# A mixture of softmaxes: 64-row units with two heads per partition, all heads weighed on TensorE, half rows stored

## The chip, the cores and the metric

The kernel runs on one core of one Trainium2 chip. The metric is the device time of one execution in microseconds (us), the median of several runs. The kernel before took 806.44 us, the median of 3 runs from 806.37 to 809.75.

## The reference

For each of 32*128 = 4096 rows there are four heads of 4096 logits and four prior values. The result is the mean of the four softmaxes, weighed with the softmax of the prior:

```python
prior_probs = softmax(prior)                    # (32, 128, 4)
sm = exp(logits - logits.max(axis=-1, keepdims=True))
sm = sm / sm.sum(axis=-1, keepdims=True)        # (32, 128, 4, 4096)
out = np.sum(prior_probs[..., None] * sm, axis=2)   # (32, 128, 4096) float32
```

The logits are 268.4 MB, the result is 67.1 MB, all in float32.

## The kernel before

**Tiling.** A unit `u` is 128 rows, one row on each partition with all four heads, 8 MB; there are 32 units. Rows are taken in groups of 256 (`g`), and partition `p` has the rows 2p and 2p+1 of a group, one in each of two units (`j`). A unit comes in two loads of 4 MB (heads 0 and 1, heads 2 and 3), each into one of four slots of [128, 2, 4096]; a load has one packet of 32 KB per partition. The loads are issued from ScalarE's queue (`load`, L63 to L68).

**Per head** (`top`, L76): VectorE finds the negated maximum of 4096 values (L77), ScalarE replaces the values by their exponentials and sums them up (L80), VectorE takes the reciprocal of the sum (L86). For heads 0 to 2, GpSimd makes a diagonal matrix of reciprocal times prior (L89), and TensorE multiplies it with the exponentials in eight pieces of 512 columns, summed up over the heads in PSUM (L95). A float32 matmul is two instructions in the profile. [...]

**The fourth head** isn't on TensorE. For columns 0 to 3071, VectorE multiplies the head by its weight and adds the accumulator, in three pieces (`merge`, L107). For the last 1024 columns ScalarE copies the accumulator (L152), GpSimd weighs the head (L146) and adds the two (L160).

**Order.** Everything is issued in an order written out by hand (`tc.manual_schedule()`); each engine works through its own instructions in order, and waits are semaphores that follow from the buffers. In the loop over `u` (L141) the finishing of unit `w = u - 1` is put between the four heads of unit `u`. The load of the second half of unit u+1 is issued after the fourth head of w is used up (L164), that of the first half of unit u+2 at the end of the round (L177).

**Stores.** Two units share one output buffer [128, 2, 4096] of two; as the two rows of a partition lie next to each other in memory, a store of 4 MB has one contiguous run of 32 KB per partition (L167), and it covers all 128 partitions. It is issued on SP's queue. The last units are stored on their own (L169, L183).

**The prior** is loaded by SP (L114, 32 partitions of 2 KB), made into a softmax by VectorE and ScalarE, and transposed in 32 x 32 blocks into `pp`, so that each partition has the prior of its row as a scalar (L125 to L139).

Of the kernel before, what the change touches and what calls it, by code (L numbers as in the profile page):

```python
# [7 lines left out]
FP32 = mybir.dt.float32  # L8
AF = mybir.ActivationFunctionType
ALU = mybir.AluOpType  # L10
AX = mybir.AxisListType

P = 128
J = 2
BANK = 512


@with_exitstack
def kernel(
    ctx: ExitStack,  # L20
    tc: tile.TileContext,
    logits: bass.AP,
    prior: bass.AP,
    out: bass.AP,
):
    nc = tc.nc
    B, S, H, V = logits.shape
    R = P * J
    G = B * S // R
    U = G * J  # L30
    assert G * R == B * S and 2 * G == 32 and H == 4 and V == 8 * BANK


    lg = logits.rearrange("b s h v -> (b s) h v").rearrange("(g p j) h v -> g j p h v", p=P, j=J)
    ov = out.rearrange("b s v -> (b s) v").rearrange("(g p j) v -> g p j v", p=P, j=J)
    pv = prior.rearrange("b s h -> (b s) h").rearrange("(k r) h -> k r h", r=P)

    cpool = ctx.enter_context(tc.tile_pool(name="cpool", bufs=1))
    psum = ctx.enter_context(tc.tile_pool(name="psum", bufs=1, space=bass.MemoryType.PSUM))


    slots = [cpool.tile([P, 2, V], FP32, name=f"slot{i}") for i in range(4)]

    obufs = [cpool.tile([P, J, V], FP32, name=f"obuf{i}") for i in range(2)]
    acc = psum.tile([P, V], FP32, name="acc")

    ident = cpool.tile([P, P], FP32, name="ident")
    diag = [cpool.tile([P, P], FP32, name=f"diag{h}") for h in range(3)]
    pr = cpool.tile([2 * G, P, H], FP32, name="pr")
    pn = cpool.tile([2 * G, H, P], FP32, name="pn")  # L50
    pmax = cpool.tile([2 * G, P], FP32, name="pmax")
    pp = cpool.tile([P, J, H, 2 * G + 1], FP32, name="pp")
    nmax = [cpool.tile([P, U], FP32, name=f"nmax{h}") for h in range(H)]
    dsum = [cpool.tile([P, U], FP32, name=f"dsum{h}") for h in range(H)]
    rden = [cpool.tile([P, U], FP32, name=f"rden{h}") for h in range(H)]
    last = cpool.tile([P, U], FP32, name="last")

    DVE_COLS = 6 * BANK

    def slot(u, h):  # L60
        return slots[(2 * u + h // 2) % 4][:, h % 2]

    def load(u, half, cuts=(0, 2)):  # L63
        for a, b in zip(cuts, cuts[1:]):
            nc.scalar.dma_start(
                out=slots[(2 * u + half) % 4][:, a:b],
                in_=lg[u // J, u % J, :, 2 * half + a : 2 * half + b, :],
            )  # L68

    def obuf(u):  # L70
        return obufs[(u // J) % 2][:, u % J]

    def prob(u, h):
        return pp[:, u % J, h, 2 * (u // J) + 1 : 2 * (u // J) + 2]

    def top(u, h):  # L76
        nc.vector.tensor_reduce(  # L77
            out=nmax[h][:, u : u + 1], in_=slot(u, h), axis=AX.X, op=ALU.max, negate=True
        )
        nc.scalar.activation(  # L80
            slot(u, h), slot(u, h), AF.Exp, bias=nmax[h][:, u : u + 1],
            accum_out=dsum[h][:, u : u + 1],
        )

    def recip(u, h):
        nc.vector.reciprocal(rden[h][:, u : u + 1], dsum[h][:, u : u + 1])  # L86

    def matmuls(u, h):
        nc.gpsimd.tensor_scalar(  # L89
            out=diag[h], in0=ident, scalar1=rden[h][:, u : u + 1], scalar2=prob(u, h),  # L90
            op0=ALU.mult, op1=ALU.mult,
        )
        for b in range(V // BANK):
            cols = slice(b * BANK, (b + 1) * BANK)
            nc.tensor.matmul(  # L95
                acc[:, cols], lhsT=diag[h], rhs=slot(u, h)[:, cols],
                start=h == 0, stop=h == H - 2,
            )

    def weight(u):  # L100
        recip(u, H - 1)
        nc.gpsimd.tensor_mul(  # L102
            last[:, u : u + 1], rden[H - 1][:, u : u + 1], prob(u, H - 1)
        )

    def merge(u, lo, hi):
        nc.vector.scalar_tensor_tensor(  # L107
            out=obuf(u)[:, lo:hi], in0=slot(u, H - 1)[:, lo:hi], scalar=last[:, u : u + 1],
            in1=acc[:, lo:hi], op0=ALU.mult, op1=ALU.add,
        )  # L110

    with tc.manual_schedule():
        load(0, 0)
        nc.sync.dma_start(out=pr, in_=pv)  # L114
        load(0, 1)
        load(1, 0)
        load(1, 1)

        nc.gpsimd.memset(ident, 1.0)  # L119
        nc.gpsimd.affine_select(  # L120
            out=ident, in_=ident, compare_op=ALU.is_equal, fill=0.0, base=0,
            pattern=[[-1, P]], channel_multiplier=1,
        )

        nc.vector.reduce_max(pmax, pr, axis=AX.X)  # L125
        nc.vector.tensor_sub(pr, pr, pmax.unsqueeze(2).to_broadcast([2 * G, P, H]))  # L126
        nc.scalar.activation(pr, pr, AF.Exp)  # L127
        nc.vector.reduce_sum(pmax, pr, axis=AX.X)  # L128
        nc.vector.reciprocal(pmax, pmax)  # L129
        nc.vector.tensor_mul(  # L130
            pn.rearrange("k h r -> k r h"), pr, pmax.unsqueeze(2).to_broadcast([2 * G, P, H])
        )
        pq = pn.rearrange("k h (p j) -> k j h p", j=J)
        for t in range(P // 32):
            c = 1 - t // 2
            nc.vector.transpose(  # L136
                pp[32 * t : 32 * (t + 1), :, :, c : c + 2 * G],
                pq[:, :, :, 32 * (t % 2) : 32 * (t % 2 + 1)],
            )  # L139

        for u in range(U):  # L141
            w = u - 1
            top(u, 0)
            if w >= 0:
                weight(w)
                nc.gpsimd.tensor_scalar(  # L146
                    out=slot(w, 3)[:, DVE_COLS:], in0=slot(w, 3)[:, DVE_COLS:],
                    scalar1=rden[3][:, w : w + 1], scalar2=prob(w, 3),
                    op0=ALU.mult, op1=ALU.mult,
                )  # L150
                merge(w, 0, 2 * BANK)
                nc.scalar.copy(obuf(w)[:, DVE_COLS:], acc[:, DVE_COLS:])  # L152
            top(u, 1)
            recip(u, 0)
            if w >= 0:
                merge(w, 2 * BANK, 4 * BANK)
                merge(w, 4 * BANK, 6 * BANK)
            matmuls(u, 0)
            if w >= 0:
                nc.gpsimd.tensor_add(  # L160
                    obuf(w)[:, DVE_COLS:], obuf(w)[:, DVE_COLS:], slot(w, 3)[:, DVE_COLS:]
                )
                if u + 1 < U:
                    load(u + 1, 1, (0, 2) if u + 1 < U - 1 else (0, 1, 2))  # L164
                if w % J == J - 1:
                    eng = nc.sync if w < U - J - 1 else nc.scalar
                    eng.dma_start(out=ov[w // J], in_=obufs[(w // J) % 2])  # L167
                elif w == U - 2:
                    nc.sync.dma_start(out=ov[w // J, :, w % J], in_=obuf(w))  # L169
            top(u, 2)  # L170
            recip(u, 1)
            matmuls(u, 1)
            top(u, 3)
            recip(u, 2)
            matmuls(u, 2)
            if u + 2 < U:
                load(u + 2, 0)  # L177

        u = U - 1
        weight(u)  # L180
        for lo in (0, V // 2):
            merge(u, lo, lo + V // 2)
            nc.sync.dma_start(  # L183
                out=ov[u // J, :, u % J, lo : lo + V // 2], in_=obuf(u)[:, lo : lo + V // 2]
            )


# [28 lines left out]
```

## Time and profile before

| | |
|---|---|
| median of 3 runs | 806.44 us |
| the profiled execution | 805.12 us |
| its span, first to last instruction | 803.4 us |
| TensorE clock granted, mean | 0.973 |
| HBM read, written | 268.5 MB, 67.1 MB |
| loads of 4 MB: issue to landing, median | 21.9 us |
| stores of 4 MB | 23.7 us |
| stores of 1 MB, at the end | 3.9 us |

The page shows busy time by engine and by group of instructions. PE is TensorE, PEld its weight loads, DVE is VectorE, ACT ScalarE, POOL GpSimd, SP SyncE, which issues transfers. In the rows of 40 slices each digit is a busy share in tenths, and GB/s is what the 16 DMA engines moved. q10 is the queue of the transfers issued from ScalarE, q1 that of those issued from SP. Beside the page, the trace has a record for each packet (one contiguous run of a transfer on one DMA engine) with its start, duration, size and queue.

### The profile page before, as it was taken

The numbers are of one execution on the slowest core, as the hardware profiler recorded it, in microseconds if no ns is written. First come the engines' busy times: TensorE is split into PE (matmuls) and PEld (weight loads), VectorE is DVE, ScalarE is ACT, GpSimd is POOL, SyncE is SP. The second block draws the span as 40 slices with busy tenths as digits, with TensorE's granted clock in tenths as the row PEclk, the third lists the DMA queues.
The fourth block names the chain that finished last, engine by engine and source line by source line (L and its number), as shares of the span: only waits on it lengthen the run. The fifth ranks groups of instructions, "written<-read, shape, count | busy, mean of one in ns | idle before, by whom it ended". The sixth has DMA issues, their size and how long they took to land.

```text
span 803.4 us, 4541 instructions
## 1 busy us (share of the span) xinstructions
PE 691.1 (86%) x1536; PEld 295.3 (37%) x1536; DVE 689.6 (86%) x360; ACT 517.0 (64%) x289; POOL 158.6 (20%) x196
## 2 busy tenths in 40 slices
PE   0899898897998979979798998979989898897996
PEld 0344343333343434334343343333434333343442
DVE  6799898798889979799798898978889897898993
ACT  2776677575675756676666766656757666575672
POOL 0112222121221212211122211212212122121220
PEclk9999999998999999999999999989999999899999
DMA  9999999999999999999999999999999999999992
GB/s 395 427 432 389 420 443 414 438 426 438 416 424 428 427 426 437 423 440 437 425 434 427 432 427 438 427 436 421 423 432 432 433 426 434 430 404 439 425 392 106
DMA packets 12023, 335.90 MB, mean 418 GB/s; under 512 B 1344, under 2 KB 1344, under 8 KB 1376
## 3 DMA queue, kind: packets, MB, share of 16 engines
q10 hardware_dynamic: 9504, 272.63, 79.4%
q1 hardware_dynamic: 2496, 62.98, 18.4%
q8 instruction: 12, 0.20, 0.1%
q14 instruction: 11, 0.09, 0.0%
HBM read 268.50 MB, written 67.11 MB: 418 GB/s over the span
## 4 chain that ended last, share of the span: by engine, by line
DMA 45%; DVE 20%; PE 19%; issue 9%; POOL 6%; ACT 0%; POOLq 0%; DVEq 0%; ACTq 0%
DMA slot<-in_logits_dram 45%; PE acc L95 19%; DVE nmax L77 17%; POOL obuf L160 4%; DVE obuf L107 3%; POOL diag L89 1%; DVE rden L86 1%; POOL last L102 0%; POOL slot L146 0%; ACT obuf L152 0%; POOLq L89 0%; ACT slot L80 0%; DVEq L107 0%; POOLq L146 0%; POOLq L160 0%
## 5 line engine op out<-in xcount | busy, mean ns | idle before, releaser
L95 PE MATMUL acc<-slot,diag 128*128 128x512 f32 x1536 | 691.1, 609 | 104.9 <-POOL diag L89 104.9
L77 DVE TENSOR_REDUCE nmax<-slot 128x1 f32<-128x4096 f32 x128 | 563.9, 4411 | 61.7 <-DMA slot<-in_logits_dram 61.7
L80 ACT ACTIVATE slot<-slot,nmax 128x4096 f32<-128x4096 f32 x128 | 474.9, 3710 | 203.7 <-DVE nmax L77 182.5
L95 PEld LDWEIGHTS acc<-slot,diag 128*128 128x128 f32 x1536 | 295.3, 195 | 499.8 <-issue 349.0
L107 DVE SCALAR_TENSOR_TENSOR obuf<-slot,last,acc 128x1024 f32<-128x1024 f32 (+1 forms) x95 | 120.5, 1295 | 37.8 <-PE acc L95 23.8
L89 POOL TENSOR_SCALAR diag<-ident,rden,pp 128x128 f32<-128x128 f32 x96 | 42.9, 447 | 490.9 <-DVE rden L86 476.6
L160 POOL TENSOR_TENSOR obuf<-obuf,slot 128x1024 f32<-128x1024 f32 x31 | 73.7, 2376 | 0.0
L152 ACT COPY obuf<-acc 128x1024 f32<-128x1024 f32 x31 | 31.4, 1012 | 63.9 <-PE acc L95 63.9
L146 POOL TENSOR_SCALAR slot<-slot,rden,pp 128x1024 f32<-128x1024 f32 x31 | 37.0, 1194 | 0.0
L102 POOL TENSOR_TENSOR last<-rden,pp 128x1 f32<-128x1 f32 x32 | 6.1, 189 | 139.7 <-DVE rden L86 139.7
L80 ACT ACTIVATION_READ_ACCUMULATOR slot<-slot,nmax 128x1 f32 x128 | 23.9, 187 | 0.0
L86 DVE RECIPROCAL rden<-dsum 128x1 f32<-128x1 f32 x128 | 19.6, 153 | 3.8 <-ACT slot L80 3.8
L125 DVE TENSOR_REDUCE pmax<-pr 32x128 f32<-32x512 f32 x1 | 0.7, 673 | 4.7 <-DMA pr<-in_prior_dram 4.7
L127 ACT ACT_TABLE_LOAD x1 | 1.3, 1283 | 3.2 <-issue 3.2
L136 DVE STREAM_TRANSPOSE pp<-pn 32x256 f32<-32x256 f32 x4 | 1.7, 434 | 0.1
L127 ACT ACTIVATE pr<-pr 32x512 f32<-32x512 f32 x1 | 0.6, 628 | 1.6 <-DVE pr L126 1.6
L128 DVE TENSOR_REDUCE pmax<-pr 32x128 f32<-32x512 f32 x1 | 0.7, 674 | 0.7 <-ACT pr L127 0.7
L130 DVE TENSOR_TENSOR pn<-pr,pmax 32x512 f32<-32x512 f32 x1 | 1.0, 1017 | 0.0
L129 DVE RECIPROCAL pmax<-pmax 32x128 f32<-32x128 f32 x1 | 0.9, 941 | 0.0
L126 DVE TENSOR_TENSOR pr<-pr,pmax 32x512 f32<-32x512 f32 x1 | 0.7, 679 | 0.0
L120 POOL TENSOR_SCALAR_AFFINE_SELECT ident<-ident 128x128 f32<-128x128 f32 x1 | 0.3, 292 | 0.1
L119 POOL MEMSET ident<- 128x128 f32 x1 | 0.2, 204 | 0.3 <-POOLq L200 0.3
(4 smaller groups left out, 0.4 us busy)
## 6 DMA issues: line engine op xcount, KB each, us to landing
slot<-in_logits_dram ACTq DMA_DIRECT2D x63, 4096.0 KB, 21.9
out_dram<-obuf SPq DMA_DIRECT2D x14, 4096.0 KB, 23.7
slot<-in_logits_dram ACTq DMA_DIRECT2D x2, 2048.0 KB, 13.4
out_dram<-obuf ACTq DMA_DIRECT2D x1, 4096.0 KB, 23.7
out_dram<-obuf SPq DMA_DIRECT2D x1, 2048.0 KB, 7.8
out_dram<-obuf SPq DMA_DIRECT2D x2, 1024.0 KB, 3.9
pr<-in_prior_dram SPq DMA_DIRECT2D x1, 64.0 KB, 3.8
```

The costliest lines, as they stand in the source:

```text
L77: nc.vector.tensor_reduce(out=nmax[h][:, u : u + 1], in_=slot(u, h), axis=AX.X, op=ALU.max, negate=True)
L80: nc.scalar.activation(slot(u, h), slot(u, h), AF.Exp, bias=nmax[h][:, u : u + 1], accum_out=dsum[h][:, u : u + 1],)
L86: nc.vector.reciprocal(rden[h][:, u : u + 1], dsum[h][:, u : u + 1])
L89: nc.gpsimd.tensor_scalar(out=diag[h], in0=ident, scalar1=rden[h][:, u : u + 1], scalar2=prob(u, h), op0=ALU.mult, op1=ALU.mult,)
L95: nc.tensor.matmul(acc[:, cols], lhsT=diag[h], rhs=slot(u, h)[:, cols], start=h == 0, stop=h == H - 2,)
L102: nc.gpsimd.tensor_mul(last[:, u : u + 1], rden[H - 1][:, u : u + 1], prob(u, H - 1))
L107: nc.vector.scalar_tensor_tensor(out=obuf(u)[:, lo:hi], in0=slot(u, H - 1)[:, lo:hi], scalar=last[:, u : u + 1], in1=acc[:, lo:hi], op0=AL ...
L127: nc.scalar.activation(pr, pr, AF.Exp)
L136: nc.vector.transpose(pp[32 * t : 32 * (t + 1), :, :, c : c + 2 * G], pq[:, :, :, 32 * (t % 2) : 32 * (t % 2 + 1)],)
L146: nc.gpsimd.tensor_scalar(out=slot(w, 3)[:, DVE_COLS:], in0=slot(w, 3)[:, DVE_COLS:], scalar1=rden[3][:, w : w + 1], scalar2=prob(w, 3), o ...
L152: nc.scalar.copy(obuf(w)[:, DVE_COLS:], acc[:, DVE_COLS:])
L160: nc.gpsimd.tensor_add(obuf(w)[:, DVE_COLS:], obuf(w)[:, DVE_COLS:], slot(w, 3)[:, DVE_COLS:])
```

## The change

A unit `n` is now 64 rows, 4 MB, one load: partition 2m + q has the heads 2q and 2q+1 of row m, 32 KB in one run. There are 64 units, five slots of 32 KB per partition, and all loads are on SP's queue. For `i` = 0 and 1 a unit has one maximum and one exponential over 128 partitions, which now cover two heads of 64 rows each.

TensorE weighs all four heads: the stationary operand `wt` is 128 x 64, with the weight of partition 2m + q in column m, so that the contraction adds the two heads of a row, and the two `i` are summed up in PSUM. The columns of the result are cut in two: the half `c` = 0 goes to PSUM partitions 0 to 63, the half `c` = 1 to partitions 64 to 127, each a matmul of its own on its own half of the array's columns. There are two accumulators of 128 x 2048. VectorE's merges and GpSimd's large instructions are gone; ScalarE copies the whole accumulator of a unit to SBUF in one instruction (`evict`).

The copy leaves half a row on a partition. So a group of two units is stored by two transfers of 1 MB (`store`), each from 64 partitions, with runs of 8 KB. They are issued from ScalarE's queue. The stores of the last four groups (`HOLD`) are issued on SP's queue behind the last load; the last two groups use a free slot as their buffer (`home`). The prior's load moves to ScalarE's queue.

```diff
-    lg = logits.rearrange("b s h v -> (b s) h v").rearrange("(g p j) h v -> g j p h v", p=P, j=J)
-    ov = out.rearrange("b s v -> (b s) v").rearrange("(g p j) v -> g p j v", p=P, j=J)
+    lg = logits.rearrange("b s h v -> (b s) h v").rearrange(
+        "(g m j) (q i) v -> g j m q (i v)", m=M, j=J, i=Q
+    )
+    ov = out.rearrange("b s v -> (b s) v").rearrange("(g m j) v -> g m j v", m=M, j=J)
...
-    slots = [cpool.tile([P, 2, V], FP32, name=f"slot{i}") for i in range(4)]
-    obufs = [cpool.tile([P, J, V], FP32, name=f"obuf{i}") for i in range(2)]
-    acc = psum.tile([P, V], FP32, name="acc")
+    slots = [cpool.tile([P, Q, V], FP32, name=f"slot{i}") for i in range(SLOTS)]
+    obuf = cpool.tile([P, 2, J, W], FP32, name="obuf")
+    accs = [psum.tile([P, W], FP32, name=f"acc{i}") for i in range(2)]
...
+    def load(n):
+        src = lg[n // J, n % J]
+        if n < N - 1:
+            nc.sync.dma_start(out=slots[n % SLOTS], in_=src)
+        else:
+            for i in range(Q):
+                nc.sync.dma_start(
+                    out=slots[n % SLOTS][:, i], in_=src[:, :, i * V : (i + 1) * V]
+                )
...
+    def weigh(n, i):
+        nc.vector.reciprocal(rden[i][:, n : n + 1], dsum[i][:, n : n + 1])
+        wt = wts[n % 2][i]
+        nc.gpsimd.tensor_scalar(
+            out=wt, in0=sel, scalar1=rden[i][:, n : n + 1],
+            scalar2=pp[:, n % J, i, n // J : n // J + 1], op0=ALU.mult, op1=ALU.mult,
+        )
+        for b in range(W // BANK):
+            for c in range(2):
+                nc.tensor.matmul(
+                    accs[n % 2][c * M : (c + 1) * M, b * BANK : (b + 1) * BANK],
+                    lhsT=wt,
+                    rhs=slots[n % SLOTS][:, i, c * W + b * BANK : c * W + (b + 1) * BANK],
+                    start=i == 0, stop=i == Q - 1,
+                )
+    HOLD = G - 4
+    def home(g):
+        if g < G - 2:
+            return obuf[:, g % 2]
+        return slots[(N - 5) % SLOTS][:, g % 2].rearrange("p (j w) -> p j w", j=J)
+    def evict(n):
+        nc.scalar.copy(home(n // J)[:, n % J], accs[n % 2])
+    def store(g, js=slice(0, J)):
+        eng = nc.scalar if g < HOLD else nc.sync
+        for c in range(2):
+            eng.dma_start(
+                out=ov[g, :, js, c * W : (c + 1) * W], in_=home(g)[c * M : (c + 1) * M, js]
+            )
...
+        for n in range(N):
+            w = n - 1
+            top(n, 0)
             if w >= 0:
+                weigh(w, 1)
+                if w + SLOTS < N:
+                    load(w + SLOTS)
+            top(n, 1)
+            weigh(n, 0)
             if w >= 0:
+                evict(w)
+                if w == N - SLOTS:
+                    for g in range(HOLD, w // J):
+                        store(g)
+                if w % J == J - 1 and (w // J < HOLD or w >= N - SLOTS):
+                    store(w // J)
+        n = N - 1
+        store(n // J, slice(0, 1))
+        weigh(n, 1)
+        evict(n)
+        store(n // J, slice(1, 2))
```

## The prediction

> **What bounds the kernel now.** I read the page's busy times and slices first, then the queues, then stretches of the span, then the groups for single durations. The page's rows of totals, slices and queues:
>
> ```profile
> PE 691.1 (86%) x1536; PEld 295.3 (37%) x1536; DVE 689.6 (86%) x360; ACT 517.0 (64%) x289; POOL 158.6 (20%) x196
> ...
> DMA  9999999999999999999999999999999999999992
> GB/s 395 427 432 389 420 443 414 438 426 438 416 424 428 427 426 437 423 440 437 425 434 427 432 427 438 427 436 421 423 432 432 433 426 434 430 404 439 425 392 106
> ...
> q10 hardware_dynamic: 9504, 272.63, 79.4%
> q1 hardware_dynamic: 2496, 62.98, 18.4%
> ```
>
> No compute engine is full, but the 16 DMA engines are in 39 of 40 slices: 79.4% and 18.4% of 803.4 us are 785.7 us of packets per engine. The stretches (columns: the stretch, its length, busy time and count of PE, PEld, DVE, ACT, POOL, then clock, DMA share, GB/s) show where the rest lies:
>
> ```profile
> 400.00:500.00 100.00, 90.43 (x204) 38.66 (x203) 88.01 (x47) 65.98 (x39) 20.88 (x26) 0.98 1.00 430
> ...
> 760.00:780.00 20.00, 18.68 (x45) 8.04 (x44) 19.03 (x10) 15.09 (x9) 4.59 (x5) 1.00 0.94 400
> 780.00:790.00 10.00, 10.00 (x25) 4.50 (x24) 5.75 (x5) 7.60 (x4) 1.08 (x3) 1.00 0.32 134
> 790.00:795.00 5.00, 5.00 (x13) 2.13 (x13) 2.33 (x1) 0.00 (x0) 0.00 (x0) 1.00 0.00 2
> 795.00:803.40 8.40, 0.99 (x3) 0.17 (x1) 2.36 (x2) 0.00 (x0) 0.00 (x0) 0.83 0.61 250
> ```
>
> The middle is transfer and nothing else (share 1.00). The idle DMA is in the end: 20*0.06 + 10*0.68 + 5 + 8.4*0.39 = 16.3 us, while the last unit is computed. So two things decide: what one packet costs, and what DMA does in the last 20 us. That the chain of waits names PE and DVE beside DMA says little here, as transfers are queued behind transfers throughout.
>
> The trace's packet records give the price of a packet on its engine: 32 KB takes 1213 ns (10th to 90th percentile, loads and stores alike), 16 KB 611, 8 KB 309 (median 314 in the last stores), so 9 ns per packet beside the bytes. In the records an engine that has both queues filled takes one load packet and one store packet in turn.
>
> **The compute, part by part.** The durations are these rows:
>
> ```profile
> L95 PE MATMUL acc<-slot,diag 128*128 128x512 f32 x1536 | 691.1, 609 | 104.9 <-POOL diag L89 104.9
> L77 DVE TENSOR_REDUCE nmax<-slot 128x1 f32<-128x4096 f32 x128 | 563.9, 4411 | 61.7 <-DMA slot<-in_logits_dram 61.7
> L80 ACT ACTIVATE slot<-slot,nmax 128x4096 f32<-128x4096 f32 x128 | 474.9, 3710 | 203.7 <-DVE nmax L77 182.5
> ...
> L152 ACT COPY obuf<-acc 128x1024 f32<-128x1024 f32 x31 | 31.4, 1012 | 63.9 <-PE acc L95 63.9
> ```
>
> A new unit moves one 4 MB load. At the DMA price it takes 803.4/64 = 12.5 us. DVE: 2*4.41 + 2*0.15 = 9.1 us (the 120.5 us of merges go). ACT: two exponentials with their read-outs, 2*(3.71 + 0.19), and a copy of 128x2048, estimated at twice 1.01 less a little, 1.9: 9.7 us, plus two 0.33 us store issues in every second unit. POOL: two small multiplies below 0.45 each; its 110.7 us of large ones go. All are below 12.5, so what they lose or gain lies beside the transfers and is worth nothing until the last load.
>
> PE: 16 matmuls of 64 columns, two instructions each; the row of back-to-back ones shows 20.87 us for 48, 0.435 each. If the two column tiles run beside each other a unit takes 16*0.435 = 7.0 us, if not 32*0.435 = 13.9, above 12.5. The trace has no column tile; both ends are kept, and I take the first, since the tiles have weights, outputs and columns of their own. [...]
>
> Waits: the last matmuls of a unit now stand behind the next unit's first reduction, so a slot comes free about 4.4 + 0.2 + 0.5 + 3.5 = 9 us (12 with serial tiles) after the next load has landed. Three loads, 37 us, are queued then; that covers it. On SP only loads wait, and stores have left that queue until the end. The PSUM copy waits for the store of two groups before, issued some 37 us earlier; with alternating packets it takes 16*(1.213 + 0.310) = 24.4 us. If that cover were gone, the exponentials behind the copy on ACT would wait, and loads two slots later. The preamble's weights move to ACT's queue and pass loads packet by packet; about 2 us late at most, covered by five loads.
>
> **The transfers.** Per engine: loads 512*1.213 = 621.1 us, as now; stores 512 packets of 8 KB at 0.310 = 158.7 instead of 128 at 1.213 = 155.3, so +3.5. The stalls of single packets (records above 1213 ns) were 8.0 us per engine, other gaps about 4, the first packet starts at 2.2.
>
> In the end the change wins: stores of the last four groups (64 packets an engine, 19.8 us) are held behind the last load. So the last load lands at T = 2.2 + 621.1 + 448*0.310 + 8 + 4 = 774.2. Then follow reduction (the first half's ends about T + 3.8), second reduction to 8.4, exponential to 12.8 (ACT also has a copy and one exponential ahead), reciprocal and weights 0.6, 8 matmuls 3.5, copy 1.9, store of 1 MB about 4 (3.9 for one of that size in the page): T + 23.5. The held stores would fit under it, if they run at 0.310 a packet.
>
> **What I don't believe is that price.** Every large transfer before covers 128 partitions; each new store covers 64. The only narrower transfer in the trace is the prior's: 32 partitions, 32 packets of 2 KB at the start. Alone such packets took 81 to 85 ns; with twelve to fifteen of them in flight, 98 to 146, median of all 89.5, and together they never moved more than about 240 GB/s, against 16*32768/1213 = 432 for the 128-partition loads. So engines that serve a narrow range of partitions seem to get in each other's way, by 1.0 to 146/82 = 1.78. A gain is excluded: no packet of 32 KB is faster than 1211 ns. For 8 KB that is 310 to 552 ns.
>
> - Between loads, where a store packet is a fifth of an engine's cycle (310 of 1523 ns) and engines are spread, I take the median, 89.5/84 = 1.07: 448*0.021 = 9.4 us; ends 0 and 448*0.242 = 108.
> - Behind the last load all engines do nothing but stores, all on the same half at a time; there I take the upper end: 64*0.552 = 35.3 us, with 2 us to land 37.3 instead of 23.5; the compute is then covered by the stores.
>
> Sum: 774.2 + 9.4 + 37.3 = 820.9 us of span. The profiled execution of before took 805.12 for a span of 803.4, 1.7 more, and stands 1.3 below the median of 806.44. **Forecast 822.6 us.**
>
> [...]
>
> **Rivals.**
> - **Narrow stores cost nothing** (other side). Prices stay at 0.310, the end is compute: 774.2 + 23.5 + 1.7 = 799.4 us, 0.7% below the profiled execution. For it: 17 of the 32 prior packets took 91 ns or less, and a load packet between two stores may give time to read ahead. It decides as long as the narrow packets lose under about 10 ns between loads and the held stores stay under 24 us.
> - **Engines in step.** If they do their store packets at the same moment, the 1.78 holds between loads too: 774.2 + 108 + 37.3 + 1.7 = 921; halfway 867. For it: at 100 us the records show 14 of 16 engines within 120 ns of each other. Against: at 700 us they are spread over the whole 1213.
> - **Column tiles run in turn.** PE then bounds: 2048*0.435 = 891 us, from 22.6 us (first matmul now) and 6 for the last copy and store: 920 + 1.7 = about 921.
>
> **How the numbers follow.** Narrow stores with a moderate price (812 to 870 us): 0.45. They cost nothing (797 to 806): 0.38. In step, beyond 870: 0.08. Tiles in turn: 0.09. The range 797 to 870 holds the first two, 0.83; the forecast's own is 812 to 870. About 0.5% is what a measurement of this kernel can tell from no change: under 802.4 I put 0.30 (most of the second case), within 802.4 to 810.5 0.08, above 0.62.
>
> **What would show it.** Packet records of 8 KB: near 310 ns throughout would refute the forecast; 330 between loads and 500 to 620 behind the last load bear it out. The GB/s of the last 40 us: about 420 or about 240. The chain that ended last: stores under the forecast, DVE, ACT and PE under the first rival. PE's back-to-back matmuls: 16 instructions in 3.5 us or in 7. DMA share below 0.95 in the middle would mean that a wait I called covered isn't, and the whole working would be wrong.

## The result, and the profile after

The changed kernel took 794.35 us (median of 4 runs, 793.69 to 795.03) beside 806.40 for the kernel before in the same job: a ratio of 0.9841, 95% interval 0.9814 to 0.9867. It is faster by 1.6%. The prediction had 822.6, a range of 797 to 870, and 0.62 for slower; the time lies below the range. Its profiled execution took 794.60 us for a span of 792.9.

The page of the changed kernel, its totals, slices, queues and chain:

```profile
PE 544.3 (69%) x2048; PEld 159.6 (20%) x2048; DVE 573.3 (72%) x268; ACT 600.1 (76%) x322; POOL 51.1 (6%) x135
...
DMA  9999999999999999999999999999999999999997
GB/s 375 441 414 431 430 426 429 433 431 428 433 436 433 434 434 431 429 427 437 429 431 429 431 434 431 433 436 430 433 432 432 427 432 427 432 431 438 432 386 234
...
q1 hardware_dynamic: 10544, 276.83, 81.9%
q10 hardware_dynamic: 8112, 58.79, 17.6%
...
DMA 76%; PE 10%; DVE 10%; issue 1%; POOL 1%; ACT 1%; SPq 0%; POOLq 0%
```

The chain of the kernel before:

```profile
DMA 45%; DVE 20%; PE 19%; issue 9%; POOL 6%; ACT 0%; POOLq 0%; DVEq 0%; ACTq 0%
```

Three things differ from before. The middle is smoother: from the fourth slice to the last but two the rate stands at 426 to 438 GB/s, where before it went down to 389, 414 and 404. The last slice moves 234 GB/s in place of 106. And the chain that ended last goes through the loads for 76% of the span, where it was 45%. No compute engine is over 76% busy; ACT has 600 us.

The groups behind the compute terms, and the transfers (last number: us from issue to landing):

```profile
L91 PE MATMUL acc<-slot,wt 128*64 128x512 f32 x2048 | 544.3, 689 | 236.6 <-POOL wt L84 236.5
...
L106 ACT COPY obuf<-acc 128x2048 f32<-128x2048 f32 x60 | 110.7, 1845 | 0.0
...
slot<-in_logits_dram SPq DMA_DIRECT2D x63, 4096.0 KB, 38.0
out_dram<-obuf ACTq DMA_DIRECT2D x56, 1024.0 KB, 25.5
```

A load lands 38.0 us after its issue, about the time of three loads, its own among them; that is the queue that the prediction counted on.

The stretches of the end (stretch, length, PE, PEld, DVE, ACT, POOL, then clock, DMA share, GB/s):

```profile
760.00:770.00 10.00, 8.54 (x40) 2.55 (x38) 10.00 (x5) 9.55 (x6) 0.79 (x2) 1.00 1.00 383
770.00:775.00 5.00, 3.62 (x19) 1.05 (x16) 2.33 (x2) 5.00 (x3) 0.39 (x1) 1.00 1.00 338
775.00:780.00 5.00, 4.96 (x26) 1.50 (x24) 0.17 (x1) 3.13 (x3) 0.39 (x1) 1.00 0.88 282
780.00:785.00 5.00, 0.87 (x6) 0.00 (x0) 0.00 (x0) 1.87 (x1) 0.00 (x0) 1.00 0.96 274
785.00:792.90 7.90, 0.00 (x0) 0.00 (x0) 0.00 (x0) 0.00 (x0) 0.00 (x0) 0.56 0.49 151
```

The last load lands at about 765. From there the DMA engines are busy (share 1.00, 0.88, 0.96), but move 270 to 340 GB/s: the share counts a packet that takes long as busy, and only GB/s tells that it does.

The packet records say the same by packet. "Long" is the sum of what packets of 8, 16 and 32 KB took above 309, 611 and 1213 ns, per DMA engine; "idle" is time with no packet from the first to the last, per engine. "Between loads" are the store packets ahead of the held ones:

```
kernel                        8 KB between loads       8 KB behind the last load   long, us   idle, us
before                        none                     median 314 (1 MB stores)    8.4        16.7
changed                       median 309, mean 309.9   mean 397, a tenth over 632  7.8        4.8
changed, wide held stores     mean 309.9               mean 311                    1.9        5.1
changed, two groups held      mean 309.9               median 627, mean 562        10.4       5.2
before, wide 8 KB stores      mean 309.8               -                           2.3        11.9
changed, three slots          mean 347                 mean 399                    77         30
```

So the narrow stores cost nothing between loads while the load queue is filled, and 28% more (397 ns against 309) behind the last load.

### The profile page after: what moved, and what is told of

It is laid out like the page before. It is cut to its first block, busy times and chain, and to the rows that moved or that the text cites. A ratio compares the mean times of both kernels' runs of the same rounds, so it can differ in the third digit from the quotient of the medians.

```text
span 792.9 us, 5418 instructions
## 1 busy us (share of the span) xinstructions
PE 544.3 (69%) x2048; PEld 159.6 (20%) x2048; DVE 573.3 (72%) x268; ACT 600.1 (76%) x322; POOL 51.1 (6%) x135
## 4 chain that ended last, share of the span: by engine, by line
DMA 76%; PE 10%; DVE 10%; issue 1%; POOL 1%; ACT 1%; SPq 0%; POOLq 0%
DMA slot<-in_logits_dram 76%; PE acc L91 10%; DVE nmax L74 9%; POOL wt L84 1%; ACT slot L77 0%; ACT slot L106 0%; SPq L65 0%; DVE rden L82 0%; POOLq L84 0%
## 5 line engine op out<-in xcount | busy, mean ns | idle before, releaser
L91 PE MATMUL acc<-slot,wt 128*64 128x512 f32 x2048 | 544.3, 689 | 236.6 <-POOL wt L84 236.5
L91 PEld LDWEIGHTS acc<-slot,wt 128*64 128x64 f32 x2048 | 159.6, 157 | 620.4 <-POOL wt L84 315.4
L106 ACT COPY obuf<-acc 128x2048 f32<-128x2048 f32 x60 | 110.7, 1845 | 0.0
L84 POOL TENSOR_SCALAR wt<-sel,rden,pp 128x64 f32<-128x64 f32 x128 | 50.3, 393 | 725.3 <-DVE rden L82 725.3
L106 ACT COPY slot<-acc 128x2048 f32<-128x2048 f32 x4 | 7.4, 1850 | 2.8 <-PE acc L91 2.8
## 6 DMA issues: line engine op xcount, KB each, us to landing
out_dram<-obuf ACTq DMA_DIRECT2D x56, 1024.0 KB, 25.5
```

The lines of the kernel that those rows point to most:

```text
L84: nc.gpsimd.tensor_scalar(out=wt, in0=sel, scalar1=rden[i][:, n : n + 1], scalar2=pp[:, n % J, i, n // J : n // J + 1], op0=ALU.mult, op1= ...
L91: nc.tensor.matmul(accs[n % 2][c * M : (c + 1) * M, b * BANK : (b + 1) * BANK], lhsT=wt, rhs=slots[n % SLOTS][:, i, c * W + b * BANK : c * ...
L106: nc.scalar.copy(home(n // J)[:, n % J], accs[n % 2])
```

## The experiments

The theory on record was that a store from 64 partitions makes its packets longer, a little between loads and by 1.78 behind them. The trace after had refuted the first half of it; the rivals that were left concern why, what the end costs, and where the 6 us of long packets in the middle went.

**How many slots.** In both, the two last groups use a buffer of their own:

```diff
-SLOTS = 5
+SLOTS = 4
```

> The changed kernel with four slots in place of five; the last two groups use a buffer of their own. Theory of depth: the 6 us of long packets that the change removed went because its load queue is never short; with four slots two loads (25 us) are still queued when a slot comes free about 10 us after the next landing, so long packets stay near 2 us per engine and the time at 794 to 796 us. Rival: it is the fifth slot that does it; then the stalls of 6 to 8 us of the kernel before come back, 799 to 802 us.

Measured: 794.46 us (794.26 to 794.99), ratio 0.9875 (0.9835 to 0.9915), as the theory of depth has it; a load lands 25.9 us after issue, and long packets in the middle are 1.9 us (2.2 with five). The fifth slot is worth nothing.

```diff
-SLOTS = 5
+SLOTS = 3
```

> The changed kernel with three slots. Theory of depth: one load (12.4 us with its share of stores) is queued when a slot comes free 9 to 10 us after a landing, and 1 to 2 us pass from issue to the first packet, so the queue runs short often: long packets or idle engines of 5 to 30 us, 800 to 825 us. Rival (depth is of no account, the stalls of before came from the size of its store packets): long packets stay near 2 us and the time below 797 us.

Measured: 887.38 us, ratio 1.1017 (1.0958 to 1.1077), far more than either forecast. Its page:

```profile
DMA  9999999999999999999999999999999999999798
GB/s 383 394 374 404 377 357 385 374 385 381 394 393 391 366 399 368 367 375 363 395 385 387 385 376 401 376 380 368 382 404 395 374 374 367 403 403 402 315 377 262
```

DMA is still at nine tenths up to the last slices, but at 360 to 400 GB/s. By the packet records engines were idle for 30 us, and load packets were long by 52 us per engine, store packets by 23. Four fifths of the long time in the middle lies in packets that began within 6 us of a moment at which at least two engines had no packet; 42% of all packets began there. The loads show it more sharply. The first five aside, 28 of 58 sent their first packet less than 1.5 us after they were issued, so that hardly anything was queued ahead of them. The first 16 packets of these 28 make 13.4 of the 16.3 us by which the first 16 of all 58 were long. An empty queue costs more than the gap: the packets after it are long too.

**Narrow stores of 32 KB in the kernel before.**

```diff
-                    eng.dma_start(out=ov[w // J], in_=obufs[(w // J) % 2])
+                    for c in range(2):
+                        rows = slice(c * 64, (c + 1) * 64)
+                        eng.dma_start(out=ov[w // J][rows], in_=obufs[(w // J) % 2][rows])
```

> The kernel before with each 4 MB store cut into two of 64 partitions, packets of 32 KB as before. [...] Rival, that a narrow store is free as long as load packets stand between (an engine reads ahead): packets stay at 1213 ns and the time within 806 +- 4 us.

Measured: 844.06 us, ratio 1.0482 (1.0435 to 1.0529): slower by 39 us, as a price on narrow packets would have it, but most of the loss isn't in them. Store packets are long by 9.8 us per engine, the wide load packets by 33.6, and idle time in the middle grows from 2.3 to 7.2 us. Where load and store packets alternated, nearly all of both kept 1213 ns (the records from 491 to 499 us, about 430 GB/s). A possible chain is that narrow stores that stand alone slow the engines unevenly, a load is complete with its slowest engine, the next is issued late, and the queue runs empty. It fits that 21 of 59 loads sent their first packet less than 2.5 us after their issue, where the kernel before has 12. The chain is argued, not shown.

**Wide stores of 8 KB in the kernel before.**

```diff
+                    for c in range(2):
+                        cols = slice(c * V // 2, (c + 1) * V // 2)
+                        eng.dma_start(
+                            out=ov[w // J][:, :, cols], in_=obufs[(w // J) % 2][:, :, cols]
+                        )
```

> The kernel before with each 4 MB store cut into two halves of the columns: packets of 8 KB, all 128 partitions. If the stalls of before came from 32 KB store packets that halve the loads' share, they shrink by 4 to 6 us and the time is 804 to 806 us with 3.5 us for 9 ns on each of 5376 more packets. If they came from a load queue that runs short, they stay and the time is 808 to 811 us.

Measured: 800.05 us (796.36 to 802.11), ratio 0.9923 (0.9893 to 0.9953). The kernel before went from 800.8 to 810.5 in that job. This is below both forecasts. In the profiled execution, the fastest (796.36), long packets fell from 8.4 to 2.3 us per engine; idle time fell too, from 16.7 to 11.9, most of it in the end, which neither theory had. Smaller store packets alone are worth about half of the whole change.

The record of issues ties the two theories together. In the kernel before, 12 of 59 loads sent their first packet less than 2.5 us after their issue, and the first packets of these 12 make 1.95 of the 2.1 us by which the first packets of all 59 were long. With stores of 8 KB it is 2 loads of 58, and most follow 4 to 9 us after their issue; in the changed kernel nearly all follow after 21 us or more. So with 32 KB store packets the load queue does run short, and part of the long time lies there.

**The same, narrow as well** (four stores, halves of rows and of columns):

> The kernel before with each 4 MB store cut in four: halves of the partitions and halves of the columns, so narrow and with packets of 8 KB. If narrow packets are free whenever load packets stand between, only those behind the last load of a burst lose: 800 to 806 us, at most 6 above the wide 8 KB version (800.05). If the loss of the narrow 32 KB version (844) came from being narrow alone, whatever the packet: 830 to 850 us.

Measured: 802.92 us, ratio 0.9967 (0.9940 to 0.9994), as the first forecast has it. Narrow and 8 KB costs 0.4% beside wide and 8 KB, by two ratios whose intervals just meet; narrow and 32 KB costs 5%. Size of packet and width of transfer have to be seen together.

**Fewer groups held.**

```diff
-    HOLD = G - 4
+    HOLD = G - 2
```

> The changed kernel with only the last two groups' stores held behind the last load. The last load lands 32 packets * 0.309 = 9.9 us later; the compute behind it, 17 us to the last copy and 4 for the last store, then covers the 32 held packets per engine even at 0.62 us each (19.8 us). Theory that the changed kernel's gain is its filled end: the time rises to 797 to 799 us. Rival, that holding is of no account because the narrow stores at the end lose what they fill: 793 to 795 us.

Measured: 797.45 us (797.22 to 797.71), ratio 0.9888 (0.9859 to 0.9917), as forecast: holding two more groups is worth 3.1 us. The records put these in long packets (10.4 us per engine for 7.8), not in idle time (5.2 and 4.8): the end is filled in both. The 32 held packets of each engine took 562 ns in the mean, yet most hid beside the compute: the last copy ends at 788.7 us, 7.3 before the end of the span.

**Held stores made wide.** Two transfers of 64 partitions become one of 128, packets of 8 KB, 32 KB apart in memory as before:

```diff
...
+        if g >= HOLD:
+            eng.dma_start(out=ow[g // 2, g % 2, :, js], in_=home(g)[:, js])
+            return
...
```

The values of these groups then stand in other places of the result. This version, the next one and the one with three slots and wide stores serve for the time alone.

> The changed kernel, but the last four groups' stores cover all 128 partitions in one transfer, with packets of 8 KB and the same pitch of 32 KB per partition in memory; for that the half rows of these groups go to other places of the result (permuted). [...] Rival, that stores without loads between run into a limit of the memory, narrow or not: packets stay long and the time at 793 to 795 us.

Measured: 789.06 us (788.77 to 789.10), ratio 0.9784 (0.9760 to 0.9808), within the 787 to 790 expected if it is the narrow range of partitions that makes the held packets long. Its end:

```profile
770.00:775.00 5.00, 3.63 (x18) 1.06 (x16) 1.81 (x2) 5.00 (x3) 0.39 (x1) 1.00 1.02 429
775.00:780.00 5.00, 4.96 (x24) 1.35 (x20) 0.16 (x1) 2.60 (x3) 0.39 (x1) 1.00 0.68 287
```

429 GB/s where the changed kernel has 338, then a share of 0.68, as engines have nothing left to store. Held packets took 311 ns in the mean. The last copy ends at 782.3 us and the span 4.8 us later; in the changed kernel it ends at 782.8, and stores go on for another 10.1. So the 23.0 us from the last load to the end are the compute's and the last store's.

**Held stores narrow, in one contiguous stretch of memory each.**

> The changed kernel, but each narrow store (64 partitions) of the last four groups goes to one contiguous stretch of the result, partition after partition at a pitch of 8 KB in place of 32 KB (permuted). [...] Rival, that the pitch in memory makes 16 engines meet in the same place: packets of 309 ns, 787 to 790 us.

Measured: 794.40 us, ratio 0.9850 (0.9826 to 0.9875); held packets 399 ns in the mean, as in the changed kernel (397). It is the range of partitions that counts, not the pitch in memory. Nor is it the size of a transfer: the 1 MB stores at the end of the kernel before, over 128 partitions, kept a median of 314 ns.

Narrow stores that have the engines to themselves run at about half the rate: with two groups held, three quarters of the 512 packets took 500 ns or more, the median 627, twice 309 and a little, and the stretch from 782 to 786 us moved 211 GB/s, where the wide held stores moved 429 (770 to 775 us). Why a narrow range does this, no run shows. Packets that stand between wide ones pay nothing of it: 309.9 ns in the mean of 7168.

**Column tiles one after the other.**

```diff
-        for b in range(W // BANK):
-            for c in range(2):
+        for c in range(2):
+            for b in range(W // BANK):
```

> The changed kernel with the loops over pieces and column tiles swapped: all matmuls of the first tile, then all of the second. If tiles run beside each other only when neighbours in the order are of different tiles, a burst of 16 instructions takes 16 * 0.435 = 7.0 us in place of 3.65, PE needs 13.9 us per unit against 12.4 for the transfers, and the time is 900 to 930 us. If TensorE looks far enough ahead to overlap them all the same, 793 to 795 us.

Measured: 793.93 us, ratio 0.9845 (0.9808 to 0.9883). The time is the rival's, but the burst is neither's: TensorE overlaps the tiles still, if less. The timelines of PE, first the changed kernel, then this one:

```profile
764.12 3.65 PE L91 MATMUL acc<-slot,wt 128*64 128x512 f32 x16 [0.73 <-POOL wt L84]
```

```profile
411.62 10.64 PE L91 MATMUL acc<-slot,wt 128*64 128x512 f32 x32 [2.34 <-POOL wt L84]
```

That is 0.228 us per instruction and 0.333, beside 0.435 in the kernel before. The second burst ran at a granted clock of 0.86 (410 to 422 us); another of this version, at 1.00 (423 to 435 us), took 9.81 us, 0.307 an instruction. At the full clock the gain is 1.9 and 1.4 times. That it is overlap, and not a cheaper instruction of 64 columns, the records of the changed kernel show: two instructions start 6 ns apart, and the next two 0.43 us later, the distance between single instructions of 128 columns before. At 10.6 us a unit PE still stays under the 12.3 of the transfers.

**Three slots, all stores wide.**

> The changed kernel with three slots and all stores over 128 partitions (half rows go to other places of the result, permuted). Theory that the loss of the three-slot version (887) is an empty load queue and the slow start after it, which has nothing to do with narrow stores: 865 to 890 us. Rival, that narrow stores running alone while no load is queued cause it: 800 to 830 us.

Measured: 848.10 us in the profiled execution, which is used here, and 872.04 in the only other. The 848.10 lie in neither forecast. The profiled execution has 27 us of idle and 38 us of long load packets per engine, and store packets of 309.4 ns. Of the 93 us that three slots lose, narrow stores then make about 40 (887.38 to 848.10), of which 5 are the end that wide stores fill (794.35 to 789.06); the greater part comes without them. Here too the first packets of loads that found the queue empty are the long ones: 23 loads of 58, sent within 1.5 us of their issue, make 12.0 of 12.9 us.

**Versions meant to be better.** With three groups held, the last three loads in halves, and the last copy split:

```diff
-    HOLD = G - 4
+    HOLD = G - 3
...
-        if n < N - 1:
+        if n < N - 3:
...
-        evict(n)
+        half = W // 2
+        nc.scalar.copy(home(n // J)[:, n % J, :half], accs[n % 2][:, :half])
+        nc.vector.tensor_copy(home(n // J)[:, n % J, half:], accs[n % 2][:, half:])
```

> A version meant to beat the changed kernel: three groups' stores held in place of four, the last three loads cut in halves so that VectorE starts on each half as it lands, and the last copy split between ScalarE and VectorE. VectorE's last reduction ends about 2 us earlier, the last copy 1 us shorter, 4.95 us of narrow stores go under the loads, so the last load lands 5 us later: 790 to 793 us. If the end is bound by the narrow stores alone and not by the compute: 792 to 795.

Measured: 793.26 us (792.95 to 793.31), ratio 0.9855 (0.9824 to 0.9885): about 1 us under the changed kernel, which the intervals of the two ratios don't tell apart. The forecast of 790 to 793 was missed by little; the time is that of an end bound by the narrow stores.

> The same with four groups held, as in the changed kernel. If the end of the changed kernel is bound by the held narrow stores, the earlier compute buys at most 1 us: 793 to 794.5 us. If it is bound by compute: 790.5 to 792.

Measured: 794.50 us, ratio 0.9874 (0.9843 to 0.9905), as the first forecast has it: an earlier compute buys nothing while the narrow stores end last.

## Why the prediction was wrong, point by point

- **The bound** was read rightly in the main: transfers before and after, and compute in their shadow, but for the 12 of 59 loads that came late in the kernel before. The copy took 1.85 us (1.9 estimated), PE's burst 3.65 (3.5), the wide end 23.0 (23.5, though the steps listed for it add up to 22.8). The rival of serial tiles did not come: 2048 instructions kept PE busy for 544 us.
- **The failed step: "the median, 89.5/84 = 1.07" between loads.** Worth 9.4 us in the sum; measured nothing (309.9 ns). The row it came from, the prior's load, was narrow packets with nothing between them, in the first us of the kernel. It could speak for the end at most, and not for a queue in which every second packet is a wide one. Nor do its records show a price of crowding: of the 18 packets that started with ten or more of them in flight, 13 took 81 to 91 ns, and of the seven that started with five or fewer, three took 98. The first rival named a reason, time to read ahead; whether that is the mechanism no run shows, only that 8 KB packets between loads are free.
- **"The stalls of single packets were 8.0 us per engine", carried over unchanged.** Worth 5.8 us: 2.2 were left in the middle. The prediction didn't ask when they came. In the trace before, about 6 of the 8 us lie in eleven clusters of six or more long packets within 3 us, mostly where transfers began or ended. The wide 8 KB version shows that the size of the store packets decides whether they come. The records fit a reason: an engine takes one packet of each queue in turn (a group's stores landed in 25.5 us, where 16 pairs of 1.52 us are 24.4), so a 32 KB store packet takes half of the engine from the loads while a store lasts, an 8 KB one a fifth, and with 32 KB the load queue ran short for 12 of 59 loads. Why a packet becomes long there is open.
- **"Other gaps about 4":** too much, worth 3.5. Packets of the two queues overlap a little, and nearly nothing was lost.
- **The end: "64*0.552 = 35.3 us".** That narrow packets get longer there was right (311 ns when wide), the size wrong: 64 held packets took 397 ns in the mean, 25.4 us, and the end 28.0 in place of 37.3. Only a quarter of them took 500 ns or more; that engines come out of the loads at different times may be why, and no run tests it. With the stores wide the end is 23.0.

These four are 9.4 + 5.8 + 3.5 + 9.3 = 28.0 us, from 820.9 to 792.9. The two prices of narrow stores are 18.7 of them, and they alone made the forecast one of a slower kernel.

The gain itself, by the packet records per engine: idle time 16.7 to 4.8, long packets in the middle about 8 to 2, against 5.6 of long packets in the end and about 3 us for more and smaller packets, part of which overlaps. The first rival had the right sign. Its 799.4 was too slow by 5: it carried the same stalls and gaps, 9.3 us too many, and had the end 4.5 us too short (23.5 for 28.0), so that it lies no farther off is in part luck.

**Open:** why load packets get long after an empty queue, which costs three slots most of their 93 us, and what the rest of the clusters with 32 KB store packets are, beside the loads that found the queue short. No run separates the memory from the engines' own order there.

## What to carry to other kernels

Where transfers bound a kernel, ask of each packet what else its engine has in the queues: in this kernel a narrow store of 8 KB packets was free between wide loads (309.9 ns) and up to twice as dear alone (median 627 with two groups held). A store's packet size set its share of an engine against the loads (half at 32 KB, a fifth at 8 KB), so cutting it paid (ratio 0.9923 for wide 8 KB stores in the kernel before) even though each packet cost 9 ns more. How long a load waits between its issue and its first packet tells whether the queue is deep enough: 21 us or more cost next to nothing here (2.2 us of long packets in the middle), under 1.5 us cost long packets (three slots: 13.4 of 16.3 us). Long packets in a trace are not noise until it is seen when they come, and DMA share has to be read together with GB/s.

## What the runs showed of the hardware that was not expected

- A load queue that runs empty costs more than the gap: three slots in place of four took the time from 794.46 to 887.38 us, with 30 us of idle per engine and a DMA share of 0.9 and more up to the last slices.
- Two column tiles of 64 run beside each other in float32 (0.228 us per instruction in place of 0.435), and in part also if all matmuls of one tile stand before those of the other (0.307 at the full clock).
- The kernel before varies more from run to run (800.8 to 810.5 us in one job) than the changed one (793.7 to 795.0, four runs). What varies is open: the version with wide 8 KB stores, with 2.3 us of long packets in its profiled execution, still went from 796.4 to 802.1.
